# A hybrid attention and recurrence block on one core: the first attention head's loads and scores put within the last pair of block products, and the recurrence values of all heads made during the attention and kept in DRAM

## The chip, the core and the metric

The kernel runs on one core of a Trainium2 chip. Five engines work from instruction queues of their own: TensorE (PE) multiplies matrices, VectorE (DVE), ScalarE (ACT) and GpSimd (POOL) work element by element, and SyncE (SP) issues transfers; POOL issues transfers as well. Each queue runs in order: an instruction that waits holds all that stands behind it on its engine. The metric is the time of one execution on the device in microseconds (us), the median of several runs.

## What is computed

One residual block on an input x of 1024 tokens by 1024 channels, in float32 (RMS norms, reshapes and heads are cut here):

```python
xn = rmsnorm(x, norm1_g)
u = xn @ w_in                      # 5632 columns
q_sb, k_sb, v_sb, f_raw, i_hg, q_hg, g_hg, gate_sb, gate_hg = split(u)
# stick-breaking attention, 8 heads of 64: z = q.k/8, strictly causal
w = exp(log_sigmoid(z) + sum over later keys before t of log(1 - sigmoid(z)))
o_sb = w @ v_sb
# HGRN2 recurrence, 4 heads of 128
f = lb + (1 - lb) * sigmoid(f_raw);  k = 1 - f
S_t = diag(f_t) S_{t-1} + k_t i_t^T;  o_t = S_t^T silu(q_t)
o_hg = rmsnorm(o_hg) * silu(g_hg)
merged = sigmoid(gate_sb + b) * (o_sb @ w_o_sb) + sigmoid(gate_hg + b) * (o_hg @ w_o_hg)
h = x + merged @ w_out
h = h + relu(rmsnorm(h) @ w_ff1)**2 @ w_ff2
out = rmsnorm(h, final_g)
```

## The kernel before, in words

Every float32 operand of a product is split into a high and a low part (names ending in h and l), and a product is made of three matmuls: high by high, low by high, high by low. Some large products are made of seven block products instead of eight. TensorE has most of the work, so the kernel is arranged to give it something to do at any moment.

In order of time, with the profile's microseconds:

1. **Start, 0 to 45.** Eight token blocks of x are loaded and normalised (`norm1`): ACT sums the squares, POOL raises them to the power (line 249 scales the sum `n_ss`, line 253 raises it: `n_y`), DVE multiplies x by it (line 640), TensorE transposes (`xnt`, line 134), and DVE makes the low parts `xnl` (line 335). `early_whole(0, nc.gpsimd)` adds four high and low parts of the first half into `xw` on POOL (line 785), 128x1024 each; `early_whole(1, nc.vector)` does the second half on DVE. Between them the stream `front` makes the first queries and keys (`pjqk`) and the attention values (`pjv`); jobs up to `j_first`, then up to `j_v`.
2. **Block products, 45 to 155.** The queries and keys of the remaining heads, in four `ProjPair` objects of seven block products each (m1, m2, m6, m5, m7, m4, m3; 12 matmuls of 128x512 each; PSUM tiles `ppX`, `ppY`). ACT and DVE split their results into `qkh` and `qkl`, and POOL stores these in DRAM (line 705).
3. **Attention, 155 to 376.** 8 heads of 8 query blocks, 64 items. `qk_load` reads a head's keys `KS` and queries `QH`, `QL` from DRAM by SP (line 139). `v_load` reads its values and the values shifted by one row into `vr` by POOL (line 676); `v_split` subtracts them on DVE (line 685) and splits the difference into `V`. For each item `scores` makes `z` (TensorE), `weights` makes `rm` (sigmoid on ACT, line 946, and a scan on DVE, line 972), `turn` transposes the weights on TensorE (`pw`) and splits them (ACT `wTh`, line 1020; DVE `wTl`, line 1026), and `values` multiplies by `V` (`po`). The scores of an item are issued two items ahead. Between items fill is issued: first the rest of `front`, then steps of a second stream `st`, whose jobs stand in a fixed order. `n_fill = 3 + 7 + 2 * 9 + 17` steps are spread evenly over the 64 items. In `st` the first jobs are raw gate columns (`pga`, `pgq`, with the weights `wga0`), then the recurrence queries, values and gates of head 0.
4. **Recurrence, 376 to 646.** For each of four heads `hg_levels` builds decayed products level by level (DVE multiplies `k`, `q` and `pp`; TensorE makes `sl`, `pk`), and `hg_tail` of the head before carries the state (`fc`, `pkv`, `pho`, `pot`). After each step of either, `st.advance` issues `FILL[h]` steps, 3.75, 3.3, 2.8, 2.6 and 3 for the phases 0 to 4. Fill here is the projections of the other heads, then the output products `pys`. `i_job(h)` makes the recurrence values i of heads h and h+1: 192 matmuls of 128x256 (`pji`), which ACT copies into the slots `v`. Before, `i_job(0)` runs in the attention and `i_job(2)` in the recurrence.
5. **Gates, output and MLP, 646 to 1504.** `gates` starts with `gX`, then come `out_start` (`pwW`), and the MLP.

What sets the order around the change is the sequence written out in the main function. It issues for the last pair `o` (the one with no `n` behind it):

```python
        o.m7()
        if n:
            n.m1()
            n.split_sums()
        else:
            qk_load(0)
            v_load(0)
            front.advance(3, j_v)
        o.m4()
        o.m3()
    v_split(0)
    scores(*items[0])
    weights(*items[0])
    front.advance(2, j_v)
    scores(*items[1])
```

Of the kernel before, what the change touches and what calls it, by code (L numbers as in the profile page):

```python
# [14 lines left out]
ALU = mybir.AluOpType  # L15
# [4 lines left out]
P = 128  # L20
T = 1024
# [4 lines left out]
HGW = 512  # L26
# [13 lines left out]
def kernel(  # L40
# [19 lines left out]
    nc = tc.nc  # L60
# [14 lines left out]
    def slot(name, dt=F32):  # L75
        return spool.tile([P, 1024], dt, tag="s", name=name)
# [11 lines left out]
    def dram(name, shape):  # L88
        return scratch.tile(shape, F32, tag=name, name=name)

    def half(name, dt=F32):
        return hpool.tile([P, 512], dt, tag="h", name=name)
# [15 lines left out]
    def after(ins, earlier):  # L108
        if earlier is not None and earlier.ins is not ins.ins:
            tc.add_manual_dep(ins.ins, earlier.ins.name, NOSYNC, reason="issue order")  # L110
        return ins
# [160 lines left out]
    last_power = [None]  # L272
# [261 lines left out]
    st, front = Stream(), Stream()  # L534
# [50 lines left out]
    def wide_unit(name, mat, c0):  # L585
        return Unit(
            name,
            [
                [
                    (  # L590
                        0,
                        256,
                        mat[k * 512 : (k + 1) * 512, c0 : c0 + 256].rearrange(
                            "(k p) c -> p k c", p=P
                        ),
                    )
                ]
                for k in range(2)
            ],
            wide=True,  # L600
        )
# [47 lines left out]
    def first_row():  # L649
        zero = half("vzero")[0:1, :]  # L650
        nc.gpsimd.memset(zero, 0.0)
        nc.gpsimd.dma_start(vrows[0:1, :], zero)
# [20 lines left out]
    def v_load(h):  # L673
        vraw[h] = slot(f"vr{h}")
        for i, cs in halves():
            nc.gpsimd.dma_start(
                vraw[h][:, cs].rearrange("p (t d) -> p t d", d=DHS),
                vrows[1 - i : T + 1 - i, h * DHS : (h + 1) * DHS].rearrange(
                    "(t p) d -> p t d", p=P
                ),  # L680
            )
# [27 lines left out]
    def qk_load(h):  # L709
        qk[h] = QH, QL, KS = tuple(slot(f"{n}{h}", F32R) for n in ("QH", "QL", "KS"))  # L710
        hi, lo = qkd[h, "h"], qkd[h, "l"]
        q, k = slice(0, DHS), slice(DHS, P)
        for t, r, src in (
            (KS, q, hi[k]), (QH, q, hi[q]), (KS, k, lo[k]), (QH, k, hi[q]), (QL, q, lo[q]),
            (QL, k, lo[q]),
        ):
            load(t[r].bitcast(F32), src)
# [63 lines left out]
    def early_whole(half_, engine):  # L781
        for kp in range(KT // 2):
            h, l = (t.bitcast(F32) for t in xn.t[half_, kp])
            early[half_, kp // 2, kp % 2] = t = slot(f"xw{half_}{kp}")
            engine.tensor_tensor(out=t, in0=h, in1=l, op=ALU.add)

    early_forms = {}

# [139 lines left out]
    def scores(h, qb):  # L928
        open_block("main")
        nk = (qb + 1) * P  # L930
        QH, QL, KS = qk[h]
        rm = slot_n(f"rm{h}_{qb}", nk)
        step = 320 if nk == 640 else 512
        for s0 in range(0, nk, step):
            m = min(nk - s0, step)
            n = max(m, 256)
            z = bank(f"z{h}_{qb}_{s0}")
            for i, Q in enumerate((QH, QL)):
                matmul(
                    z[:, :n],  # L940
                    Q[:, qb * P : (qb + 1) * P],
                    KS[:, s0 : s0 + n],
                    start=i == 0,
                    stop=i == 1,
                )
            nc.scalar.activation(rm[:, s0 : s0 + m], z[:, :m], AF.Sigmoid, scale=-0.125)  # L946
        zs[h, qb] = rm
# [123 lines left out]
    def f_epilogue(h):  # L1071
# [15 lines left out]

        return ep

    def i_job(h):  # L1090
        unit = wide_unit(f"wi{h}", W_IN, C_I + h * P)

        def ep(ps, tb):
            for j in range(2):
                if tb == 0:
                    hg[h + j, "v"] = slot(f"v{h + j}")
                nc.scalar.copy(hg[h + j, "v"][:, tb * P : (tb + 1) * P], ps[:, j * P : (j + 1) * P])

        unit.late = h == 0

        def body():
            for i, _ in enumerate(token_steps(f"pji{h}", unit, xn, range(NT), ep)):
                yield
                if unit.late and i == 6:
                    hi_behind[0] = turn_hi[0]
                    st.prefetch()
                    hi_behind[0] = None

        return st.add([unit], body)

    def silu_epilogue(h, key):
        def ep(ps, half):
# [8 lines left out]
    def hg_job(h, key):  # L1121
        c0, ep = {
            "f": (C_F, f_epilogue), "q": (C_QH, lambda h: silu_epilogue(h, "q")),
            "g": (C_GH, lambda h: silu_epilogue(h, "g")),
        }[key]
        if key == "g" and h % 2 == 0:
            i_job(h)
        u = cols_unit(f"w{key}{h}", [(W_IN, c0 + h * P, P)])
        j_hg[h] = proj_jobs([(f"pj{key}{h}", u, ep(h))], xn)

# [37 lines left out]
    def chunks(t):  # L1168
        return t.rearrange("p (c t) -> p c t", t=P)
# [406 lines left out]

    j_raw = [raw_job(0)]
    hg_job(0, "q")
    hg_job(0, "g")
    j_first_hg = j_hg[0]  # L1580
    for h in range(1, NHG):
# [730 lines left out]
    norm_transpose(xn, 0, 2, 2)  # L2312
    front.advance(5, 1)
    norm1(range(4, NT))
    early_whole(0, nc.gpsimd)
    front.advance(4, 1)
    norm_transpose(xn, 1, 0, 4)
    turns["on"] = False
# [1 line left out]
    lower_bounds()  # L2320
    front.advance(11, j_first)
    first_row()
    early_whole(1, nc.vector)
    early_sums()
    blocks = [qk_parts(h) for h in range(1, NHS)] + [(((C_F, P),), f_epilogue(0))]
# [7 lines left out]
    for o, n in zip(proj, proj[1:] + [None]):  # L2333
        o.m2()
        if n:
            n.load()
        o.m6()
        o.m5()
        if n:
            n.split_plain()  # L2340
        o.m7()
        if n:
            n.m1()
            n.split_sums()
        else:
            qk_load(0)
            v_load(0)
            front.advance(3, j_v)
        o.m4()
        o.m3()  # L2350
    v_split(0)
    scores(*items[0])
    weights(*items[0])
    front.advance(2, j_v)
    scores(*items[1])

    n_fill = 3 + 7 + 2 * 9 + 17
    n_first = 0
    ready = deque()
    wsums = out_weight_sums()  # L2360
# [41 lines left out]
    for h in range(NHG + 1):  # L2402
        lev = hg_levels(h) if h < NHG else iter(())
        tail = hg_tail(h - 1) if h > 0 else iter(())
        upto = (j_hg[2], j_hg[3], j_raw[6], j_sb[1], j_sb[3])[h]
        going = True
        while going:
            going = False
            for g in (lev, tail):
                if next(g, StopIteration) is not StopIteration:  # L2410
                    going = True
                    owed += FILL[h]
                    st.advance(int(owed), upto)
                    owed -= int(owed)
        if h + 1 < NHG:
            st.finish(j_hg[h + 1])
        if h > 1:
            a_hg.put(h - 2, ohg[h - 2], hg_level[0])
# [102 lines left out]
```

## Time and profile before

| what | value |
|---|---|
| median of 3 runs | 1504.18 us (1503.21 to 1505.15) |
| the profiled execution's own time | 1505.72 us |
| its span | 1504.0 us |
| TensorE busy | 1444.2 us, 96% |
| VectorE busy | 1101.0 us, 73% |
| ScalarE busy | 658.6 us, 44% |
| GpSimd busy | 171.9 us, 11% |
| granted TensorE clock, mean | 0.982 of full speed |

The profile's times are those of one execution, in microseconds from the span's start; the 1.7 us between the span and the execution's time lie outside the program's instructions. A row of the timeline gives start, duration, engine, line, operation, output<-inputs, and in brackets how long the engine had been idle before it and what ended that. A row of the windows gives the busy time of each engine in a stretch and the granted TensorE clock (PEclk; 0.50 is half speed).

### The profile page before, as it was taken

How to read it: one execution, taken by the hardware profiler on the slowest of the kernel's cores; microseconds unless marked ns; L12 is line 12 of the kernel's file. 1: busy time of each engine (PE TensorE's matmuls, PEld its weight loads, DVE VectorE, ACT ScalarE, POOL GpSimd, SP SyncE). 2: the span in 40 equal slices, each digit the busy share in tenths (PEclk: the TensorE clock that was granted, in tenths of full speed). 3: DMA queues.
4: the chain of work that ended last, by engine and by line, in shares of the span. 5: the costliest groups of instructions: out<-in, count | busy, mean ns of one | idle time of the engine just before them, and what ended most of it. 6: DMA issues, size and time to landing. Idle time of an engine off the chain costs nothing. (4 is left out here: it accounts for less than half of the span.)

```text
span 1504.0 us, 19848 instructions
## 1 busy us (share of the span) xinstructions
PE 1444.2 (96%) x7422; PEld 1227.2 (82%) x7422; DVE 1101.0 (73%) x1538; ACT 658.6 (44%) x1080; POOL 171.9 (11%) x310
## 2 busy tenths in 40 slices
PE   7999679999999999999998999999999999999998
PEld 7988668897889888888886888888888888888886
DVE  5964568888964779887875889766666756859756
ACT  5443346655231334443333475444444534343433
POOL 5212212131000011210001030000000000000032
PEclk9999888999999999999999999999999999999999
DMA  5255655674121144874448652444444886666835
GB/s 196 85 147 168 154 155 138 136 140 92 43 91 30 54 108 152 234 231 154 150 158 256 227 182 79 139 154 154 154 155 154 310 315 235 222 236 244 286 109 192
DMA packets 164729, 248.80 MB, mean 165 GB/s; under 512 B 26860, under 2 KB 95000, under 8 KB 164632
## 3 DMA queue, kind: packets, MB, share of 16 engines
q1 hardware_dynamic: 146392, 195.87, 40.2%
q0 software_dynamic: 14496, 45.10, 10.9%
q10 hardware_dynamic: 3744, 6.56, 1.2%
q8 instruction: 58, 0.95, 0.3%
q14 instruction: 39, 0.32, 0.1%
HBM read 179.33 MB, written 72.35 MB: 167 GB/s over the span
## 5 line engine op out<-in xcount | busy, mean ns | idle before, releaser
L154 ACT CAST whid<-w 128x1024 fp32r<-128x1024 f32 x30 | 31.6, 1055 | 153.6 <-PE pm L131 85.8
L972 DVE TENSOR_TENSOR_SCAN rm<-rm,bits 128x512 f32<-128x512 f32 (+6 forms) x72 | 87.5, 1224 | 11.6 <-ACT rm L946 11.4
L131 PE MATMUL pm<-whid,sh 128*128 128x512 f32 x240 | 93.4, 389 | 0.0
L131 PE MATMUL pm<-wlod,sh 128*128 128x512 f32 x240 | 93.4, 389 | 0.0
L131 PE MATMUL pm<-whid,sl 128*128 128x512 f32 x240 | 93.4, 389 | 0.0
L131 PE MATMUL pm<-tl,sh 128*128 128x512 f32 (+1 forms) x210 | 81.3, 387 | 0.0
L131 PE MATMUL pm<-th,sl 128*128 128x512 f32 (+1 forms) x210 | 81.3, 387 | 0.0
L131 PE MATMUL pm<-th,sh 128*128 128x512 f32 (+1 forms) x210 | 81.3, 387 | 0.0
L159 DVE TENSOR_TENSOR wlod<-w,whid 128x1024 fp32r<-128x1024 f32 x30 | 36.7, 1224 | 57.5 <-ACT whid L154 57.5
L159 DVE TENSOR_TENSOR sl<-sa,sh 128x1024 fp32r<-128x1024 f32 x56 | 68.3, 1220 | 0.7 <-ACT sh L154 0.7
L2132 POOL TENSOR_SCALAR fss<-fss 128x1 f32<-128x1 f32 x8 | 4.4, 553 | 562.1 <-ACT fsc L2127 561.6
L1020 ACT ACTIVATE wTh<-pw,minus_one 128x128 fp32r<-128x128 f32 (+3 forms) x96 | 54.2, 587 | 27.4 <-PE pw L134 25.0
L154 ACT CAST sh<-sa 128x1024 fp32r<-128x1024 f32 x56 | 57.3, 1048 | 6.1 <-DMA sa<-ad 6.1
L134 PE MATMUL pw<-ident,rm 128*128 128x128 f32 x288 | 46.4, 286 | 11.9 <-DVE rm L972 11.9
L1026 DVE SCALAR_TENSOR_TENSOR wTl<-pw,wTh 128x128 fp32r<-128x128 f32 (+3 forms) x96 | 50.6, 546 | 9.7 <-ACT wTh L1020 9.3
L131 PEld LDWEIGHTS pm<-wlod,sh 128*128 128x128 f32 x240 | 45.1, 188 | 9.4
L131 PEld LDWEIGHTS pm<-whid,sl 128*128 128x128 f32 x240 | 45.0, 188 | 9.4
L131 PEld LDWEIGHTS pm<-whid,sh 128*128 128x128 f32 x240 | 45.1, 188 | 9.3
L134 PEld LDWEIGHTS pw<-ident,rm 128*128 128x128 f32 x288 | 36.8, 148 | 16.8 <-DVE rm L972 12.6
L131 PE MATMUL po<-wTh,V 128*128 128x256 f32 x160 | 45.5, 312 | 5.1 <-DVE wTl L1026 3.3
L131 PE MATMUL pX<-sql,t1h 128*128 128x512 f32 x128 | 50.0, 391 | 0.1
L131 PE MATMUL pX<-sqh,t1l 128*128 128x512 f32 x128 | 49.8, 389 | 0.0
(963 smaller groups left out, 4613.4 us busy)
## 6 DMA issues: line engine op xcount, KB each, us to landing
w<-in_w_ff_dram SPq DMA_DIRECT2D x72, 512.0 KB, 5.1
sa<-ad SPq DMA_DIRECT2D x56, 512.0 KB, 6.2
ad<-a SPq DMA_DIRECT2D x32, 256.0 KB, 4.2
ad<-s SPq DMA_DIRECT2D x16, 512.0 KB, 5.9
tw<-in_w_out_dram POOLq DMA_DIRECT2D x24, 256.0 KB, 5.2
x<-in_x_dram SPq DMA_DIRECT2D x8, 512.0 KB, 8.7
qkh<-qkh POOLq DMA_DIRECT2D x16, 256.0 KB, 3.2
qkl<-qkl POOLq DMA_DIRECT2D x16, 256.0 KB, 3.2
```

Of the source, the lines that this page charges most:

```text
L131: return pe(nc.tensor.matmul(*a, **k))
L134: return pe(nc.tensor.transpose(dst, src, ident))
L154: hi_last[0] = after(in_turn("act", nc.scalar.copy(dst, src)), hi_behind[0])
L159: nc.vector.tensor_tensor(out=dst, in0=src, in1=hi.bitcast(F32), op=ALU.subtract),
L972: sc = nc.vector.tensor_tensor_scan(out=rr, data0=rr, data1=bits[:, 1024 - nk + a : 1024 - nk + b][:, ::-1], initial=rm[:, b : b + 1] if i ...
L1020: nc.scalar.activation(th[:, 0:n, qs], src, AF.Identity, bias=minus_one),
L1026: nc.vector.scalar_tensor_tensor(out=tl[:, 0:n, qs], in0=src, scalar=-1.0, in1=th[:, 0:n, qs].bitcast(F32), op0=ALU.add, op1=ALU.subtract,),
L2132: nc.gpsimd.tensor_scalar(out=ssq, in0=ssq, scalar1=1.0 / D, scalar2=EPS, op0=ALU.mult, op1=ALU.add)
```

## The change

Three things are changed.

- `early_whole(0, nc.gpsimd)`, POOL's four additions `xw`, is called later, behind `first_row()`, and each is ordered behind POOL's last power step (`last_power`).
- For the last pair, `qk_load(0)` and `v_load(0)` stand behind m6 instead of m7, the first item's `scores` and `weights` stand between m4 and m3, and all that is left of the attention values (`front`) is issued behind m3, around the scores of the second item.
- Both `i_job` calls stand in `st` behind the first head's recurrence queries. An `i_job` no longer copies into the slots `v`: ACT copies a 128x256 result into one half of a 128x512 tile, and POOL stores each full tile in the DRAM tensor `irows` (8 stores of 256 KB). A new `i_load(h - 1)` reads one head's values back (512 KB, POOL) at the start of phase h. `n_fill` goes from 45 to 59; `FILL` stays.

```diff
         for kp in range(KT // 2):
             h, l = (t.bitcast(F32) for t in xn.t[half_, kp])
             early[half_, kp // 2, kp % 2] = t = slot(f"xw{half_}{kp}")
-            engine.tensor_tensor(out=t, in0=h, in1=l, op=ALU.add)
+            after(engine.tensor_tensor(out=t, in0=h, in1=l, op=ALU.add), last_power[0])
...
+    irows = dram("irows", [T, HGW])
+
     def i_job(h):
         unit = wide_unit(f"wi{h}", W_IN, C_I + h * P)
+        pair = {}
 
         def ep(ps, tb):
-            for j in range(2):
-                if tb == 0:
-                    hg[h + j, "v"] = slot(f"v{h + j}")
-                nc.scalar.copy(hg[h + j, "v"][:, tb * P : (tb + 1) * P], ps[:, j * P : (j + 1) * P])
+            i, c = tb // 2, tb % 2 * 256
+            if c == 0:
+                pair[i] = half(f"i{h}_{i}")
+            nc.scalar.copy(pair[i][:, c : c + 256], ps)
+            if c:
+                rows_ = irows[i * 256 : (i + 1) * 256, h * P : (h + 2) * P]
+                nc.gpsimd.dma_start(
+                    rows_.rearrange("(t p) c -> p t c", p=P),
+                    pair.pop(i).rearrange("p (t c) -> p t c", t=2),
+                )
...
+    def i_load(h):
+        hg[h, "v"] = slot(f"v{h}")
+        nc.gpsimd.dma_start(
+            chunks(hg[h, "v"]),
+            irows[:, h * P : (h + 1) * P].rearrange("(t p) c -> p t c", p=P),
+        )
...
-        if key == "g" and h % 2 == 0:
-            i_job(h)
...
     hg_job(0, "q")
+    i_job(0)
+    i_job(2)
     hg_job(0, "g")
...
     norm1(range(4, NT))
-    early_whole(0, nc.gpsimd)
     front.advance(4, 1)
...
     first_row()
+    early_whole(0, nc.gpsimd)
     early_whole(1, nc.vector)
...
         o.m6()
+        if not n:
+            qk_load(0)
+            v_load(0)
         o.m5()
...
-        else:
-            qk_load(0)
-            v_load(0)
-            front.advance(3, j_v)
         o.m4()
+        if not n:
+            scores(*items[0])
+            weights(*items[0])
         o.m3()
     v_split(0)
-    scores(*items[0])
-    weights(*items[0])
-    front.advance(2, j_v)
+    front.advance(4, j_v)
     scores(*items[1])
-
-    n_fill = 3 + 7 + 2 * 9 + 17
+    front.advance(5, j_v)
+
+    n_fill = 7 + 2 * 9 + 2 * 17
...
+        if h > 0:
+            i_load(h - 1)
```

The rows below, of POOL at the start of the program, are the first place at which the order differs. `n_5`, `n_6`, `n_7` are the token blocks 5 to 7; `_ss` and `_y` are the two steps of the power. Before:

```order
L253 TENSOR_TENSOR n_5_y<-n_5_ss,expo 128x1
L785 TENSOR_TENSOR xw_474<-xnh_245,xnl_246 128x1024
L249 TENSOR_SCALAR n_6_ss<-n_6_ss 128x1
L785 TENSOR_TENSOR xw_476<-xnh_253,xnl_254 128x1024
L253 TENSOR_TENSOR n_6_y<-n_6_ss,expo 128x1
L249 TENSOR_SCALAR n_7_ss<-n_7_ss 128x1
L785 TENSOR_TENSOR xw_478<-xnh_261,xnl_262 128x1024
L253 TENSOR_TENSOR n_7_y<-n_7_ss,expo 128x1
L785 TENSOR_TENSOR xw_480<-xnh_269,xnl_270 128x1024
L705 DMA qkh_99<-qkh_0_482 128x512
```

The same place on POOL in the changed kernel:

```order
L253 TENSOR_TENSOR n_5_y<-n_5_ss,expo 128x1
L249 TENSOR_SCALAR n_6_ss<-n_6_ss 128x1
L253 TENSOR_TENSOR n_6_y<-n_6_ss,expo 128x1
L249 TENSOR_SCALAR n_7_ss<-n_7_ss 128x1
L253 TENSOR_TENSOR n_7_y<-n_7_ss,expo 128x1
L705 DMA qkh_99<-qkh_0_475 128x512
L705 DMA qkl_100<-qkl_0_476 128x512
L666 DMA vrows<-v_1_518 128x2x256
L785 TENSOR_TENSOR xw_750<-xnh_246,xnl_247 128x1024
L785 TENSOR_TENSOR xw_752<-xnh_254,xnl_255 128x1024
L785 TENSOR_TENSOR xw_754<-xnh_262,xnl_263 128x1024
L785 TENSOR_TENSOR xw_756<-xnh_270,xnl_271 128x1024
```

The four additions no longer stand between the power steps of the token blocks 5 to 7; they stand behind three stores.

The second place is DVE around the first head's `vr`, at the end of the block products (`pv` is a sum of block products, `k` and `pp` belong to the forget gate, `qkl_1` is a low part to be stored, `rm_7` the first item's weights, `rm_0` and `rm_6` the next items'; the scans of line 972 are called SCALAR_TENSOR_TENSOR here and TENSOR_TENSOR_SCAN in the profile). Before:

```order
L882 TENSOR_TENSOR pv_1562<-pu_1355,ppY_1445 128x512
L1076 TENSOR_SCALAR k_1475<-k_1475,oml 128x512
L1079 TENSOR_SCALAR pp_1474<-pp_1474,oml,lb 128x512
L685 TENSOR_TENSOR vr_1489<-vr_1489 128x512
L972 SCALAR_TENSOR_TENSOR rm_0_1610<-rm_0_1610,bits 128x128
L159 TENSOR_TENSOR V_1569<-vr_1489,V_1569 128x8x64
L972 SCALAR_TENSOR_TENSOR rm_7_1572<-rm_7_1572,bits 128x512 x2
L972 SCALAR_TENSOR_TENSOR rm_6_1616<-rm_6_1616,bits 128x896
```

In the changed kernel:

```order
L882 TENSOR_TENSOR pv_1485<-pu_1483,ppY_1458 128x512
L685 TENSOR_TENSOR vr_1455<-vr_1455 128x512
L1076 TENSOR_SCALAR k_1488<-k_1488,oml 128x512
L1079 TENSOR_SCALAR pp_1487<-pp_1487,oml,lb 128x512
L159 TENSOR_TENSOR qkl_1_1506<-ppX_1343,qkh_1_1505 128x512
L972 SCALAR_TENSOR_TENSOR rm_7_1511<-rm_7_1511,bits 128x512
L159 TENSOR_TENSOR V_1541<-vr_1455,V_1541 128x8x64
L972 SCALAR_TENSOR_TENSOR rm_7_1511<-rm_7_1511,bits 128x512
L882 TENSOR_TENSOR pv_1534<-pu_1356,ppY_1458 128x512
```

The subtraction `vr` stands behind the sum of m7's result instead of the one of m3's, ahead of `k`, `pp` and `qkl_1`; the first item's scans come directly behind, ahead of m3's `pv`. On POOL the load of `vr` now stands ahead of the stores of `qkh_1` and `qkl_1`, which belong to m4; before, it stood behind them. On PE the two score matmuls `z_7` with `QH` stand directly behind m7 and those with `QL` behind m4.

The third place is TensorE near the end of the last recurrence head's levels (`pys` are the output products that serve as fill; `sl_6` is the last level, `pk` the transposes that follow). Before:

```order
L131 MATMUL pys_0_6047<-asbh_5959,wo00h_5899 128x512
L131 MATMUL pys_0_6047<-asbl_5960,wo00h_5899 128x512
L131 MATMUL pys_0_6047<-asbh_5959,wo00l_5900 128x512
L134 MATMUL pk_0_6069<-ident,k_5141 128x128 x4
L134 MATMUL pk_1_6075<-ident,k_5141 128x128 x3
```

In the changed kernel:

```order
L131 MATMUL pys_1_6122<-asbh_5869,wo01h_5899 128x512
L131 MATMUL pys_1_6122<-asbl_5870,wo01h_5899 128x512
L131 MATMUL pys_1_6122<-asbh_5869,wo01l_5900 128x512
L131 MATMUL sl_6_6169<-q_5176,k_5065 64x64 x8
L134 MATMUL pk_0_6193<-ident,k_5065 128x128 x4
L134 MATMUL pk_1_6199<-ident,k_5065 128x128 x3
```

Before, 12 `pys` matmuls stand between `sl_6` and `pk_0`; in the changed kernel there are none. Between the last transposes `pot` and the first `gX` stand 78 `pys` matmuls before and 12 in the changed kernel.

## The prediction on record

> **What bounds the kernel now.** I read the page first. The span is 1504.0 us and TensorE is busy for all but 60 us of it:
>
> ```profile
> span 1504.0 us, 19848 instructions
> ...
> PE 1444.2 (96%) x7422; PEld 1227.2 (82%) x7422; DVE 1101.0 (73%) x1538; ACT 658.6 (44%) x1080; POOL 171.9 (11%) x310
> ```
>
> So an edit gains only where TensorE waits or where its clock is low. The windows by stage, in which the columns behind the span are the busy times of TensorE, its weight loads, VectorE, ScalarE and GpSimd, say where that is:
>
> ```profile
> core 0: us, PE busy (x) PEld busy (x) DVE busy (x) ACT busy (x) POOL busy (x), PEclk, DMA share, GB/s
> 0.00:45.00 45.00, 33.42 (x237) 31.98 (x238) 26.94 (x40) 25.65 (x50) 23.41 (x38) 0.89 0.58 188
> 45.00:74.00 29.00, 29.00 (x221) 27.81 (x220) 28.61 (x37) 13.97 (x22) 4.33 (x7) 1.00 0.26 73
> 74.00:155.00 81.00, 81.00 (x378) 67.86 (x378) 43.78 (x58) 31.17 (x45) 16.53 (x30) 1.00 0.51 151
> 155.00:206.00 51.00, 32.42 (x195) 28.88 (x195) 33.02 (x44) 22.73 (x48) 9.66 (x25) 0.82 0.52 132
> 206.00:376.00 170.00, 154.81 (x1009) 138.89 (x1009) 141.38 (x203) 100.23 (x222) 39.63 (x91) 0.95 0.64 138
> 376.00:417.00 41.00, 41.00 (x242) 34.45 (x241) 37.80 (x86) 10.71 (x17) 0.00 (x0) 1.00 0.14 39
> 417.00:490.00 73.00, 73.00 (x504) 66.14 (x504) 42.29 (x87) 20.47 (x54) 3.07 (x5) 1.00 0.20 62
> 490.00:559.00 69.00, 69.00 (x396) 58.53 (x395) 48.69 (x97) 21.52 (x45) 5.75 (x7) 1.00 0.25 69
> 559.00:622.00 63.00, 61.27 (x362) 52.00 (x361) 57.01 (x103) 24.53 (x47) 12.97 (x16) 1.00 0.70 194
> 622.00:664.00 42.00, 42.00 (x215) 35.54 (x214) 35.49 (x44) 20.88 (x40) 7.78 (x11) 1.00 0.61 206
> ```
>
> TensorE is idle for 11.6 us in 0–45, 18.6 us in 155–206 and 15.2 us in 206–376. Those are also the stretches with a granted clock below 1.00. The block products (74–155) and the recurrence (376–664) leave it next to nothing, and the MLP isn't touched by the change. The summary of TensorE's waits names the causes:
>
> ```profile
> PE pw L134 <- DVE rm L972: 11.9, 2, 11.2
> ...
> PE xnt L134 <- DVE x L640: 7.5, 2, 5.4
> ...
> PE pga L131 <- ACT wga0whi L154: 4.9, 1, 4.9
> ...
> PE pgq L131 <- ACT wga0t L154: 1.8, 1, 1.8
> ...
> PE sl L131 <- DVE pp L167: 1.7, 1, 1.7
> ...
> PE pga L131 <- DVE wga0wlo L159: 0.8, 1, 0.8
> ```
>
> Behind the long waits the clock halves. The windows show 0.50 or 0.51 there:
>
> ```profile
> 163.80:174.10 10.30, 3.24 (x15) 3.24 (x16) 6.21 (x7) 3.33 (x7) 0.00 (x0) 0.50 0.99 250
> 191.10:198.00 6.90, 5.83 (x19) 4.66 (x20) 5.41 (x8) 0.95 (x2) 0.00 (x0) 0.51 0.25 74
> 204.80:208.20 3.40, 3.40 (x9) 2.62 (x10) 1.95 (x3) 1.12 (x2) 0.00 (x0) 0.51 0.68 223
> 34.10:44.40 10.30, 4.88 (x22) 4.61 (x23) 7.39 (x7) 3.34 (x5) 7.08 (x6) 0.50 0.29 89
> ```
>
> A stretch at half clock loses half of TensorE's busy time in it: 1.6, 2.9, 1.7 and 2.4 us.
>
> **Startup.** These are GpSimd's rows around the additions `xw`, and VectorE's for the token blocks that wait for the power `n_y`:
>
> ```profile
> 27.25 2.41 POOL L785 TENSOR_TENSOR xw<-xnh,xnl 128x1024 f32<-128x1024 f32 x1
> ...
> 30.34 2.37 POOL L785 TENSOR_TENSOR xw<-xnh,xnl 128x1024 f32<-128x1024 f32 x1
> ...
> 34.13 2.34 POOL L785 TENSOR_TENSOR xw<-xnh,xnl 128x1024 f32<-128x1024 f32 x1
> 36.43 0.55 POOL L253 TENSOR_TENSOR n_y<-n_ss,expo 128x1 f32<-128x1 f32 x1
> 36.94 2.34 POOL L785 TENSOR_TENSOR xw<-xnh,xnl 128x1024 f32<-128x1024 f32 x1
> ```
>
> ```profile
> 33.25 0.75 DVE L640 TENSOR_SCALAR x<-x,n_y 128x1024 f32<-128x1024 f32 x1 [3.04 <-POOL n_y L253]
> 37.01 2.82 DVE L640 TENSOR_SCALAR x<-x,n_y 128x1024 f32<-128x1024 f32 x1 [3.01 <-POOL n_y L253]
> ```
>
> Block 7's `n_y` comes at 36.43 because three rounds of `xw` (2.41, 2.37 and 2.34 us) stand ahead of it on GpSimd. Without them it comes 7.1 us earlier, before TensorE asks for it (34.1, where its half-clock window begins), so both waits for `x` (7.5 us) go and the half-clock loss (2.4 us) with them. The upper bound of the gain is 9.9 us; VectorE must still normalise the blocks one behind another at 0.75 us, so I take 9 as the gross gain.
>
> What is late next is `xw` itself. Its four additions, 4 x 2.36 = 9.4 us, now run beside VectorE's low parts and half-1 sums. The normalisation at 37.01 took 2.82 us beside an `xw`, and the same operation at 33.25 took 0.75 us: those two did not overlap at all. Behind it, in 45–74, VectorE is busy 28.61 of 29.00 us, so what it loses there TensorE loses too. Bounds: hold of 0 (gain 9) to all of 9.4 (loss 0.4). The pair of rows shows it for one operation only; whether the low parts and the sums are held like it, no row shows. In 0–45 VectorE is busy 26.9 us of 45, so a part of a hold falls into time that it has free. I take a hold of 3, a third: **−6 (−9 to +0.5)**.
>
> The Trainium skill, SBUF — State Buffer, section "Who interferes with whom", says that a VectorE operation with at most one SBUF input, outside its two-port modes, does not contend with GpSimd, while one with two SBUF inputs shuts out a GpSimd read. By it the low parts hide about two of the four `xw`, and two, 4.7 us, are left as hold: a gain of about 4 and a sum of 1475. No run here shows it yet.
>
> **The first stall, 11.2 us before `pw`.** GpSimd's queue, VectorE's wait, two rows of TensorE (the first matmul behind m7, and the first transpose of weights), SyncE's issues, and the times from issue to landing of `vr`:
>
> ```profile
> 153.13 0.54 POOL L705 DMA_DIRECT2D qkh<-qkh  x1 [13.24 <-ACT qkh L154]
> ...
> 154.39 1.80 POOL L676 DMA_DIRECT2D vr<-vrows  x2
> ```
>
> ```profile
> 167.22 0.69 DVE L685 TENSOR_TENSOR vr<-vr 128x512 f32<-128x512 f32 x1 [9.84 <-DMA vr<-vrows]
> ```
>
> ```profile
> 144.94 0.28 PE L131 MATMUL pjv<-wv1h,xnh 128*128 128x256 f32 x1
> ```
>
> ```profile
> 170.86 0.90 PE L134 MATMUL pw<-ident,rm 128*128 128x128 f32 x3 [11.15 <-DVE rm L972]
> ```
>
> ```profile
> 138.33 0.52 SPq L139 DMA_DIRECT2D KS<-qkh  x1
> 139.47 0.45 SPq L139 DMA_DIRECT2D QH<-qkh  x1
> ```
>
> ```profile
> DMA to landing us min/median/max: 3.8/9.0/11.5
> ```
>
> GpSimd waited 13.24 us for ScalarE's `qkh` of m4 and only then issued `vr` (154.39). VectorE stood at the subtraction until 167.22 with the first head's scans behind it, and TensorE at `pw` until 170.86. In the changed kernel `vr` stands ahead of that store. It waits only for m6's buffers, so it can issue at about 140 and lands, by the slowest load (11.5 us), at 151.5. Scores come at m7's end (144.9). After them TensorE has m4 and m3, 24 matmuls of 0.22 us (74–155: 378 in 81.0 us), 5.3 us, and 96 `pjv` matmuls of half that size, 10.6 us: until about 161. From the subtraction to `pw` it took 3.6 us (167.22 to 170.86), so even the slowest `vr` has the weights ready by 156, with some 5 us to spare. The stall goes whole, with its half clock: 11.2 + 1.6 = **−12.8 (−5 to −12.8)**. The cover are those `pjv`; without them the wait would come back by the part that `vr` lands behind 151. The upper end takes that in.
>
> The price is a new wait: `z_7` stands on TensorE directly behind m7 with m4, m3 and the `pjv` queued behind it. The keys leave at 138.33 and the queries at 139.47, already as early as m6's buffers come free. No row shows these loads under a wait at this place; the nearest is `vr`, 3.8 to 11.5 us. From 139.5 that ends between 143 and 151, and TensorE asks at 144.9: 0 to 6 us. Whole rows of keys should be nearer to the fast end, so I take **+1 (0 to +6)**.
>
> **The second stall.** `wga0`'s waits (4.9, 0.8 and 1.8 us) and the half clock behind them (2.9 and 1.7) come from ScalarE's cast of weights whose load SyncE issued behind both heads' keys and queries, and whose split stood behind the first head's work. The changed SyncE order has `wga0` ahead of the second head's keys, and the splits run behind m3's sum. **−12 (−8 to −12).** Ends: all, or the half clock of the last part stays.
>
> **The rest of the attention.** 206–376 loses 15.2 us idle and 5% of 154.8 at low clock, 22.9 in all. Into it comes the second `i_job`:
>
> ```profile
> L131 PE MATMUL pji<-wi2h,xnh x64: 277/283/366, 452.8 to 481.7; 128*128 128x256 f32 x64
> ```
>
> Three such groups of 64 matmuls are 192; at half of 0.22 to 0.24 us, for half the columns, they are 21 to 23 us, and I take 22. Fill goes from 45 to 59 steps, so there are more matmuls between an item's transposes and its products. VectorE has 141.4 us in this stretch and TensorE 147 + 22 = 169 at full clock (154.8 x 0.95, and the new ones), so TensorE stays the bound, with VectorE at 83%. The waits won't all go: many are one item's chain. I let a little over half remain: **−10 (−3 to −16)**, apart from the moved work. The eight stores to `irows` stand on GpSimd in front of the memory sets for later items; those are issued well ahead of use, so nothing for them.
>
> **The recurrence and the gates.** The 22 us leave this stretch, where TensorE was busy for 286 of 288 us; that only returns if VectorE's chain lets TensorE go faster. VectorE's busy time is 37.8 of 41, 42.3 of 73, 48.7 of 69, 57.0 of 63: the phases of heads 1 and 2 have room, head 3's has none. With equal `FILL` the stock is used up earlier. Before, output products were left over:
>
> ```profile
> 645.95:663.76 17.81, 17.81 (x81) 14.72 (x80) 15.05 (x18) 8.10 (x10) 2.24 (x4) 1.00 0.75 248
> ```
>
> That block of 17.8 us, TensorE alone, covered the sums for the gates. In the changed kernel it is 12 matmuls, 2.7 us; the sums now run beside head 3's levels, on a VectorE that is full there. By the order's count at 0.22 us each TensorE has some 54 us there, against 57–59 of VectorE: +4. No fill stands between `sl_6` and `pk`: +2 (a like wait, `sl` on `pp`, cost 1.7). One half-clock window behind such waits: +1. The last head's values, 512 KB from DRAM by GpSimd, wait for a buffer that VectorE frees only behind that head's levels, and `pkv` asks for them soon after; nearest are `vr`'s 3.8 to 11.5 us, of which some 3 to 5 are covered, so +1.5 (0 to +6), nearer to the short end. Sum **+8.5 (+3 to +16)**.
>
> The Trainium skill, DMA: Bandwidth & Descriptors, section "Anatomy of one DMA", gives 2.0 us plus bytes by 436 GB/s for such a load, an estimated 3.2 us here; by it the last term would be 0. The `vr` row (9.0 us at the median for half the bytes) disagrees.
>
> **The sum.** −6 − 12.8 + 1 − 12 − 10 + 8.5 = −31.3 us. Against the profiled execution, 1505.72 us, that is 1474.4; the median lies 1.5 us below that execution, so 1473.
>
> **The rivals.**
>
> - *`xw` holds VectorE for all its 9.4 us* (for: the 2.82 us row; against: a hold of `xnl` isn't shown). The start gains nothing: 1479. Chance 0.15.
> - *The recurrence gives most back.* With the fill thinner, every phase waits for its own chain of levels; for: 57.0 of 63 busy, 17.8 us of cover gone; against: no waits in 417–559 before. The stretch keeps its length, +22 instead of +8.5: 1486. Chance 0.15.
> - *Everything is taken*: start 9, attention 16, recurrence +3 gives 1459. Chance 0.10.
> - *The early loads are not early.* The keys already left at 138.33, and `vr` could wait for something else on its queue; the first stall stays: 1486. Chance 0.05.
> - *Slower.* GpSimd's queue stops at each `irows` store until ScalarE's copy, as it did 13.24 us for `qkh`, and the next head's `vr` stands behind. Each head hit would pay what the first stall did, 12.8 us. Below two heads the change still gains; from three on (38 us) it is slower than before: 1511, and with four 1524. Against: the loads are issued a head ahead. Chance 0.05.
>
> The forecast itself, within 1465 to 1480, has 0.50. About 0.2% (3 us) is what a measurement of this kernel can tell from no change; only mixtures of the last three rivals come near it. So faster 0.92, same 0.03, slower 0.05. The range, 1459 to 1488, reaches over the second and third rival.
>
> **What would show it.** Right: TensorE's waits list no `x`, no `wga0` and no `rm` over 2 us; `vr` issues near 140 less what the start gained; PEclk is 1.00 up to 206; 622–664 loses its block of `pys`. The steps fail one by one if `z<-QH` shows over 2 us, if VectorE's `xnl` or sums last over twice as long as before beside `xw`, if `sl`, `pk` or `pkv` waits over 10 us in sum. The forecast is wrong altogether if `po` and `pw` wait as long as before with the fill denser.

## The result, and the profile after

The changed kernel takes 1493.72 us (median of 4 runs, 1493.46 to 1495.09) against 1504.66 us before (1503.21 to 1509.27): a ratio of 0.9924, 95% interval 0.9901 to 0.9946. It is faster by 11 us, where 31 were forecast, and lies above the range of 1459 to 1488. The profiled execution took 1493.49 us, its span 1491.8 us.

The page's first lines:

```profile
span 1491.8 us, 19878 instructions
...
PE 1440.0 (97%) x7422; PEld 1223.7 (82%) x7422; DVE 1106.6 (74%) x1538; ACT 656.4 (44%) x1064; POOL 177.2 (12%) x322
```

TensorE is idle for 51.8 us of the span, 8 us less than before, and its mean clock rose from 0.982 to 0.985, by estimate worth 4 us of its 1440. The summary of its waits names other causes than before; the columns are the wait, the total, the number and the longest:

```profile
PE ppar L215 <- DVE xnl L335: 9.0, 1, 9.0
PE z L131 <- DMA QH<-qkh: 8.0, 2, 4.4
...
PE sl L131 <- DVE pp L167: 4.0, 1, 4.0
PE po L131 <- ACT wTh L1020: 3.7, 3, 1.9
PE pw L134 <- ACT i L1100: 3.5, 1, 3.5
PE po L131 <- DVE wTl L1026: 2.7, 5, 1.0
PE pgq L131 <- ACT wga0t L154: 2.5, 1, 2.5
...
PE pk L134 <- DVE k L167: 1.4, 1, 1.4
```

The two big stalls at the attention's head (`rm` 11.2 us, `wga0whi` 4.9 us) are gone, and `xnt` on `x` (7.5 us) as well. The many short waits of `po` for `wTl` went from 9.9 us, in this row of before, to 2.7:

```profile
PE po L131 <- DVE wTl L1026: 9.9, 13, 3.3
```

In the place of all these stand one wait of 9.0 us for `xnl`, two for queries (8.0 us together), one for ScalarE's copy `i` (3.5 us). The windows by stage, to be read against those of before:

```profile
0.00:45.00 45.00, 32.17 (x241) 30.90 (x242) 31.92 (x40) 27.41 (x53) 24.14 (x38) 0.93 0.62 197
...
155.00:206.00 51.00, 47.37 (x301) 42.08 (x301) 38.09 (x51) 28.52 (x58) 13.31 (x31) 0.97 0.59 165
206.00:376.00 170.00, 155.66 (x1118) 145.24 (x1117) 134.00 (x186) 99.24 (x213) 42.37 (x94) 0.97 0.63 137
...
417.00:490.00 73.00, 73.00 (x413) 61.59 (x411) 45.19 (x91) 20.16 (x43) 5.63 (x7) 1.00 0.26 80
...
559.00:622.00 63.00, 57.72 (x339) 48.37 (x337) 57.91 (x97) 25.85 (x48) 13.56 (x18) 0.97 0.74 203
```

The start still loses as much as before (12.8 us idle of 45, 11.6 before). 155–206 lost only 3.6 us instead of 18.6, while 206–376 still has 14.3 us idle, 15.2 before, at a clock of 0.97 instead of 0.95. In the recurrence only the phase of the last head (559–622) waits, and there VectorE is busy 57.9 of 63.

For the comparison of all kernels I cut the span at three places that every profile shows: the last matmul of m7 in the last pair, the first `sd` (the recurrence begins), and the first `gX`. The forecast by the same stages is worked out from its terms: −6 for the start, −12.8 + 1 − 12 − 10 + 22 for the attention, −22 + 8.5 for the recurrence.

| kernel | start to m7's end | attention | recurrence to gX | rest | median, us |
|---|---|---|---|---|---|
| before | 144.9 | 230.8 | 288.1 | 840.2 | 1504.66 |
| forecast | 138.9 | 219.0 | 274.6 | 840.2 | 1473 |
| after | 145.6 | 235.1 | 271.6 | 839.5 | 1493.72 |

The recurrence came out as forecast, 3 us better. The start missed its 6 us and the attention 16 us. Those two are what the experiments are about.

### The profile page after: what moved, and what is told of

It reads as the page before. It is cut to its first block, busy times and chain, and to the rows that moved or that the text cites. A ratio compares the mean times of both kernels' runs of the same rounds, so it can differ in the third digit from the quotient of the medians.

```text
span 1491.8 us, 19878 instructions
## 1 busy us (share of the span) xinstructions
PE 1440.0 (97%) x7422; PEld 1223.7 (82%) x7422; DVE 1106.6 (74%) x1538; ACT 656.4 (44%) x1064; POOL 177.2 (12%) x322
## 5 line engine op out<-in xcount | busy, mean ns | idle before, releaser
L1020 ACT ACTIVATE wTh<-pw,minus_one 128x512 fp32r<-128x512 f32 (+2 forms) x96 | 53.4, 585 | 24.7 <-PE pw L134 23.9
L1026 DVE SCALAR_TENSOR_TENSOR wTl<-pw,wTh 128x512 fp32r<-128x512 f32 (+2 forms) x96 | 49.9, 545 | 7.5 <-ACT wTh L1020 6.9
L131 PE MATMUL pX<-sqh,t1h 128*128 128x512 f32 x128 | 49.8, 389 | 0.0
L946 ACT ACTIVATE rm<-z 128x512 f32<-128x512 f32 (+3 forms) x96 | 44.0, 492 | 6.4 <-PE z L131 4.2
```

What stands on the lines that cost most here:

```text
L131: return pe(nc.tensor.matmul(*a, **k))
L1020: nc.scalar.activation(th[:, 0:n, qs], src, AF.Identity, bias=minus_one),
L1026: nc.vector.scalar_tensor_tensor(out=tl[:, 0:n, qs], in0=src, scalar=-1.0, in1=th[:, 0:n, qs].bitcast(F32), op0=ALU.add, op1=ALU.subtract,),
```

## The experiments

**Theories.** For the start: the four additions `xw`, now back to back on GpSimd, hold one VectorE operation with two operands in SBUF, `wv1l`, and everything behind it in VectorE's queue. These are the rows of GpSimd, VectorE and TensorE of the changed kernel:

```profile
32.70 9.25 POOL L785 TENSOR_TENSOR xw<-xnh,xnl 128x1024 f32<-128x1024 f32 x4
```

```profile
29.71 0.75 DVE L640 TENSOR_SCALAR x<-x,n_y 128x1024 f32<-128x1024 f32 x1 [0.72 <-POOL n_y L253]
...
30.98 12.05 DVE L159 TENSOR_TENSOR wv1l<-wv1r,wv1h 128x1024 fp32r<-128x1024 f32 x2
42.96 4.03 DVE L335 SCALAR_TENSOR_TENSOR xnl<-xnt,prm,xnh 128x512 fp32r<-128x512 f32 x6
```

```profile
43.75 0.32 PE L215 MATMUL ppar<-ident,prow 36*128 36x36 f32 x1 [9.01 <-DVE xnl L335]
```

The last normalisation begins at 29.71, as the forecast had it, 7.3 us earlier than before (37.01). Then two `wv1l` take 12.05 us instead of the 2.35 that the same pair took before. GpSimd runs `xw` from 32.70 to 41.95, and VectorE is free again at 43.0, one `wv1l` later. The low parts `xnl` stand behind it, and TensorE waits 9.01 us for them. The pair in the profile of before:

```profile
40.35 2.35 DVE L159 TENSOR_TENSOR wv1l<-wv1r,wv1h 128x1024 fp32r<-128x1024 f32 x2
```

The rival was that GpSimd's reads hold every VectorE operation, so that no order of these would help.

For the attention: the stalls that the last pair's part removes are truly gone, but the denser fill moves its own weight loads to moments at which they hold a queue. The rival was that TensorE is simply full there.

**The cause of the start.** In the changed kernel, one small read of `wv1l` by GpSimd is put ahead of `xw`:

```diff
     first_row()
+    g0 = small.tile([P, 1], F32, tag="g0", name="g0", bufs=1)
+    w = front.jobs[j_v - 1][0][0].hl[1][1].bitcast(F32)[:, 0:1]
+    last_power[0] = nc.gpsimd.tensor_tensor(out=g0, in0=w, in1=w, op=ALU.add)
     early_whole(0, nc.gpsimd)
```

> The changed kernel with one small addition on GpSimd that reads VectorE's low part wv1l ahead of the four additions xw, so that these start only when wv1l is done. Theory (the four xw in a row hold the VectorE operation that reads two operands from SBUF, here the second wv1l, 10.9 us instead of 1.2, and the low parts xnl queue behind it): wv1l takes 1.2 us, the xnl rows run beside xw at their own 0.7 us, TensorE's wait of 9.0 us before ppar falls below 1, and the time is 6 to 8 us below the changed kernel's, 1486 to 1488. Rival (GpSimd's reads hold every VectorE operation): the hold moves to xnl, the wait stays at 7 us or more, the time stays at 1493 within 1.5.

Its rows on GpSimd and VectorE:

```profile
36.26 9.43 POOL L785 TENSOR_TENSOR xw<-xnh,xnl 128x1024 f32<-128x1024 f32 x4
```

```profile
32.84 2.35 DVE L159 TENSOR_TENSOR wv1l<-wv1r,wv1h 128x1024 fp32r<-128x1024 f32 x2
35.11 4.04 DVE L335 SCALAR_TENSOR_TENSOR xnl<-xnt,prm,xnh 128x512 fp32r<-128x512 f32 x6
...
43.15 2.58 DVE L226 TENSOR_TENSOR lmx<-prm 128x4 f32<-128x4 f32 x1
```

`wv1l` takes 2.35 us for two again, and six `xnl` run in 4.04 us, 0.67 each, the later four beside `xw`: these are not held. Only `lmx`, a tiny operation with two operands in SBUF, is held, 2.58 us until `xw` ends at 45.7. The 9.0 us wait is gone, and m7 ends at 140.5 instead of 145.6, although the later token blocks came 1.9 us later in this execution (the normalisation of block 4 began at 27.17 instead of 25.31). So the theory holds. The time, 1490.84 us (1486.87 to 1492.42; ratio to before 0.9916, 0.9889 to 0.9944), is 3 us below the changed kernel's, less than the 6 to 8 expected, and doesn't by itself separate the two; the trace does. In its profiled execution, the slowest of the four, the recurrence and the rest took 3.6 us longer than in the changed kernel. A later pair of kernels that differs by this edit alone, 1480.06 and 1474.47, agrees; another, 1485.55 and 1482.19, differs by the move of `xw` as well.

**The three parts alone.** Each is put into the kernel before by itself; the edits are hunks of the change's diff.

The move of `xw`:

> The kernel before with only the move of the four additions xw. Theory: the whole gain of the start is eaten by the hold of wv1l, so the time is that of before within 2 us, 1503 to 1506. Rival (my forecast's term, a third of the hold costs): 6 us faster, 1498.

It took 1503.26 us, ratio 0.9999 (0.9979 to 1.0019), and m7 ends at 145.2; TensorE's wait of 9.0 us for `xnl` is there too. The part gains nothing: theory.

The part on the last pair, with `n_fill = 7 + 2 * 9 + 17`:

> The kernel before with only the part on the last pair (loads behind m6, first scores between m4 and m3, attention values behind m3; 42 fill steps in place of 45, since three steps are made earlier). Theory: this part carries nearly all of the gain; the stalls of 11.2 us and 4.9 us go, a wait of some 3 us for the first queries and one of 2 us for wga0t come: 12 to 18 us below before, 1486 to 1492. Rival (it is the denser fill that removes the stalls): at most 8 us below before, 1496 or more.

It took 1485.55 us, ratio 0.9891 (0.9864 to 0.9918): 19 us faster than before, a little more than the 12 to 18 expected, and 8 us faster than the whole change. Its attention lasts 210.0 us instead of 230.8, and what is left of its waits is small and spread:

```profile
PE po L131 <- DVE wTl L1026: 10.8, 14, 1.4
...
PE pgq L131 <- ACT wga0t L154: 2.3, 1, 2.3
...
PE z L131 <- DMA QH<-qkh: 1.4, 1, 1.4
```

The forecast had −12.8 + 1 − 12 = −23.8 for this part, and 20.8 came.

The part on the recurrence values, with `n_fill = 3 + 7 + 2 * 9 + 2 * 17`:

> The kernel before with only the part on the recurrence values (both jobs in the attention, through DRAM, 62 fill steps). Theory (the denser fill pays in the attention with late loads what it saves in the recurrence): within 4 us of before, 1500 to 1508, with waits for QH or weights of 3 us and more in the attention. Rival (the forecast: waits of the attention filled, recurrence shorter by most of what moved): 10 us below before or more, 1494 or less.

It took 1503.44 us, ratio 0.9995 (0.9980 to 1.0010): nothing gained. The attention grows by 13.2 us to 244.0, which is the moved 22 us less 9, and the recurrence shrinks by 16.0. The terms are near the forecast's (10 and 13.5). By these, +12 and −13.5, this part alone was worth only 1.5 us, so the result agrees with the forecast's sum; the 10 us that the expectation puts down to the forecast aren't in it. The long waits are still there, and `wTh` has grown from 1.7 us to 6.3:

```profile
PE pw L134 <- DVE rm L972: 10.4, 1, 10.4
...
PE po L131 <- ACT wTh L1020: 6.3, 3, 2.8
PE pga L131 <- ACT wga0whi L154: 5.5, 1, 5.5
```

The sign of the theory, waits of 3 us and more for `QH` or for weights that weren't there before, didn't come: TensorE's list has no wait for queries, and `wga0whi` cost 4.9 us before.

So the parts alone give −1, −19 and −1 us, while together they give −11. Put on top of the last pair's part, the values cost the attention 25.1 us (210.0 to 235.1), all of what moved and 3 us more, instead of the 12 of the forecast. Something stands there that neither part has alone.

**What stands there.** The changed kernel's rows of SyncE, with the landing times of the queries:

```profile
200.27 1.50 SPq L139 DMA_DIRECT2D wi2r<-in_w_in_dram  x2
201.94 0.45 SPq L139 DMA_DIRECT2D KS<-qkh  x1
202.48 0.65 SPq L139 DMA_DIRECT2D QH<-qkh  x1
```

```profile
DMA to landing us min/median/max: 3.5/5.7/12.4
```

The rows of ScalarE and TensorE behind them, and two windows:

```profile
270.79 1.04 ACT L154 CAST wg0h<-wg0r 128x1024 fp32r<-128x1024 f32 x1 [6.78 <-DMA wg0r<-in_w_in_dram]
```

```profile
272.16 0.55 PE L134 MATMUL pw<-ident,rm 128*128 128x128 f32 x3 [3.51 <-ACT i L1100]
```

```profile
200.00:210.00 10.00, 10.00 (x66) 9.00 (x65) 8.67 (x14) 6.06 (x14) 2.78 (x7) 1.00 0.95 231
...
270.00:280.00 10.00, 6.42 (x30) 6.02 (x31) 6.83 (x10) 5.43 (x12) 3.05 (x9) 0.69 0.08 27
```

The second job's weights `wi2r`, 1 MB in two loads, leave at 200.27 directly ahead of head 2's keys and queries, in a window where the DMA engines are 95% busy; a load of `QH` takes up to 12.4 us, and TensorE waits 4.40 us for it at 216.36. Later ScalarE has the cast `wg0h` in its queue 6.78 us ahead of its data, with a copy `i`, a cast `V` and the `wTh` of an item behind it; TensorE waits 3.51 us, then 1.4 us, and runs at half clock behind that (0.69 in 270–280; 0.50 from 273.9 to 280.3, where it is busy for 5.6 us and so loses 2.8). With the values alone neither stands: there `wi2r` left 8 us ahead of the next head's keys, and ScalarE waited 0.30 us at `wg0h`. Two kernels take one cause each, or both.

The second values job behind the gates:

```diff
     i_job(0)
-    i_job(2)
     hg_job(0, "g")
-    j_first_hg = j_hg[0]
+    i_job(2)
+    j_first_hg = len(st.jobs)
```

> The changed kernel with the second values job behind the first head's recurrence gates in the order of the fill (queries, values of heads 0 and 1, gates, values of heads 2 and 3), so that one weight load of 512 KB, not two, stands on SyncE ahead of the keys and queries of head 2. Theory (the denser fill brings its weight loads into the same moments as the next head's queries, and the split of wg0 holds ScalarE until its load lands): the waits of 4.4 us for QH of head 2 and of 3.5 us for ScalarE's i fall below 1.5 us each, and with the half clock behind them the time is 5 to 9 us below the changed kernel's, 1485 to 1489. Rival (the added matmuls themselves are the cost, TensorE is simply full): 1492 to 1495.

```profile
PE po L131 <- DVE wTl L1026: 4.3, 7, 1.1
...
PE z L131 <- DMA QH<-qkh: 3.0, 2, 2.9
...
PE z L131 <- DMA QL<-qkl: 1.2, 1, 1.2
```

```profile
DMA to landing us min/median/max: 3.6/4.7/9.4
```

It took 1480.06 us, ratio 0.9841 (0.9818 to 0.9864), 14 us below the changed kernel: more than the 5 to 9 expected. No wait for `i` is left, and head 2's queries cost 1.4 us, 1.2 for `QL` and 0.2 for `QH`; of the 3.0 us for `QH`, 2.9 are the first head's. TensorE is idle 12.3 us in the attention instead of 21.6, at a clock of 1.00 instead of 0.96; 219.5 us is the forecast's 219.0. TensorE was not full; the rival falls.

The second cause alone, the preparation of the next weights put six steps into either job:

```diff
-        unit.late = h == 0
+        unit.late = True
```

> The changed kernel with the preparation of the next weights put six steps into the second values job as well, so that ScalarE's split of wg0 stands behind later attention work; the load order on SyncE ahead of head 2 is as in the changed kernel. Theory: the wait of 3.5 us for ScalarE's i and the 1.4 us behind it go, with their half clock 5 us: 1487 to 1490; the wait of 4.4 us for QH of head 2 stays. Rival (another instruction holds ScalarE's queue in its place): 1492 to 1495.

It took 1485.18 us, ratio 0.9876 (0.9849 to 0.9904), 2 us below the expected 1487 to 1490. The hold of ScalarE is gone, the wait for head 2's queries stays, 4.5 us of these:

```profile
PE z L131 <- DMA QH<-qkh: 4.7, 2, 4.5
...
PE po L131 <- ACT wTh L1020: 1.2, 3, 0.5
```

The attention is 10.2 us shorter. Some 2.2 of these are not the edit's: the first head's queries, ahead of which nothing was changed, cost 1.4 us here (0.3 for `QH`, 1.1 for `QL`) instead of 3.6. The other 8 fit the hold of 3.5 + 1.4 us with the 2.8 lost at half clock behind it.

The load of the first head's `vr` behind m4:

```diff
             qk_load(0)
-            v_load(0)
         o.m5()
...
         o.m4()
         if not n:
+            v_load(0)
```

> The changed kernel with the load of the first head's vr behind m4 instead of directly behind the queries. Theory (vr's transfers share the DMA engines with the first head's queries): z's first wait for QH falls from 3.6 us to 1.5 or less, vr lands by 162, before V is needed at 170, and the time is 2 to 4 us below the changed kernel's, 1490 to 1492. Rival (the queries take their time by themselves): the wait stays at 3 us or more and the time at 1493 to 1495.

The first wait for `QH` is 1.30 us here instead of 3.61, as the theory had it. But in the kernels that leave `vr` directly behind the queries this wait runs from 0.26 us to 3.61, so that `vr` takes the engines from them is not shown. Head 2's wait became 5.21 us, and the time, 1493.26 us (ratio 0.9931, 0.9904 to 0.9957), is that of the changed kernel, as the rival had it:

```profile
146.51 0.73 PE L131 MATMUL z<-KS,QH 128*128 128x512 f32 x2 [1.30 <-DMA QH<-qkh]
```

```profile
212.62 0.77 PE L131 MATMUL z<-KS,QH 128*128 128x512 f32 x1 [5.21 <-DMA QH<-qkh]
```

**The versions that come out of it.** The last pair's part with `xw` behind `wv1l`, without the values:

> The kernel before with the part on the last pair and the move of xw behind wv1l (the small GpSimd read of the first experiment), without the part on the recurrence values. Theory (the parts add, since they stand in different stages: the start 5 to 7 us, the last pair 19): 1477 to 1481. Rival (what the start gains is waited for again at the first queries): 1484 to 1487, with z waiting for QH by 5 us or more.

1482.19 us (1478.97 to 1485.02), ratio 0.9856 (0.9828 to 0.9885); m7 ends at 140.1, and the first `z` waits 0.9 us for `QH`. The start's gain is kept, though the median is 1 us above the 1481 expected at most.

The changed kernel with both corrections:

> The changed kernel with both corrections: xw behind wv1l, and the second values job behind the first gates. Theory (the two holds stand in different stages, 5 us at the start and 14 in the attention): 1473 to 1476, the start up to the end of m7 near 140 us, attention near 219, recurrence near 271. Rival (what the start gains is lost again to the first queries, or the gain of the second was chance): 1479 to 1482.

```profile
PE po L131 <- DVE wTl L1026: 4.4, 7, 1.1
...
PE sl L131 <- DVE pp L167: 4.0, 1, 4.0
PE z L131 <- DMA QH<-qkh: 3.6, 2, 2.0
...
PE pk L134 <- DVE k L167: 1.6, 1, 1.6
```

1474.47 us (1472.73 to 1477.34), ratio 0.9809 (0.9785 to 0.9833): 29 us below before. Its stages are 138.8, 220.6 and 273.2 us, against 138.9, 219.0 and 274.6 of the forecast.

Three kernels go on from this one. The first changes the rates of the fill, so that output products are left for the last head's levels:

```diff
-    FILL = (3.75, 3.3, 2.8, 2.6, 3)
+    FILL = (3.6, 3.0, 2.6, 2.8, 3)
```

> As the kernel before it, with FILL 3.6, 3.0, 2.6, 2.8, 3 in place of 3.75, 3.3, 2.8, 2.6, 3, so that 18 output products stand between sl_6 and pk of the last head, where there were none. Theory (the last head's levels wait only because the fill is used up): the waits sl on pp (4.0) and pk on k (1.4) go, 3 to 6 us below that kernel. Rival (VectorE is the bound of that phase, and the order of the fill doesn't matter): the waits move to other products, within 1.5 us of it.

1477.01 us, ratio 0.9826 (0.9805 to 0.9848), no gain: 2.5 us above the kernel it starts from, where the theory had 3 to 6 below and the rival at most 1.5 off. The wait of 4.0 us for `pp` shrinks to 1.4 and another comes:

```profile
PE pkv L131 <- DMA v<-irows: 3.2, 1, 3.2
...
PE sl L131 <- DVE pp L167: 1.4, 1, 1.4
```

That is the last head's values from DRAM: what doesn't wait at `sl` waits at `pkv`. The theory, that the missing fill alone is the cause, falls; of the rival the part holds that the wait moves on, though it moved to a transfer.

`vr` behind m4, on top of both corrections:

> As e9, with the load of the first head's vr behind m4. Theory: the first wait for QH (2.9 us there) falls to 1.5 or less as it did in the kernel with this edit alone, and now it pays: 1 to 2 us below e9. Rival: vr, later, makes VectorE's first scans late, and the time stays or rises by up to 2 us.

1474.88 us, ratio 0.9813 (0.9789 to 0.9837). The first wait for `QH` goes from 1.98 us to 0.24, the time does not move by more than the measurement tells. The next kernel, which leaves `vr` ahead, has 0.37 us there, so this wait doesn't settle it either.

The values kept in SBUF instead of DRAM (ScalarE copies into the slots `v` as before, both jobs still in the attention):

> As e9, but the values stay in SBUF: ScalarE copies 128x128 pieces into the four slots v as before the change, nothing goes through DRAM. Theory (the trip through DRAM is free, its stores have no one waiting behind them and its loads land in 6 us at most): within 2 us of e9. First rival (the trip costs transfers that slow the next head's queries): 3 us or more below e9. Second rival (four more slots held in the attention make loads wait for buffers): 5 us or more above e9.

1484.85 us, ratio 0.9882 (0.9855 to 0.9908), 10 us above the kernel with DRAM:

```profile
PE z L131 <- DMA QL<-qkl: 6.1, 3, 4.0
```

One wait for `QL` late in the attention, at 334, is 3.98 us, and TensorE is idle 17.7 us in the attention instead of 11.9. So the trip through DRAM is not what it costs; it pays, as the second rival had it. Its reason, that loads wait for the slots, wasn't shown by itself; what the trace shows is that `QL` takes 10.6 us at the median to land here, and 7.0 in the kernel with DRAM.

## Why the prediction was wrong, step by step

- **The start, −6: wrong.** The failed step is "I take a hold of 3, a third". The normalisations did come 7 us earlier, and both waits for `x` went; the wait of 9.0 us for `xnl` that came in their place brought a half clock of its own (0.50 in 45–48). The hold was not 3 us but 9.7 (12.05 − 2.35), and one operation took all of it. I looked at how much of VectorE's work would fall beside `xw` and not at which operation heads its queue there: `wv1l`, two operands in SBUF, with all the low parts behind it. The rival with the full hold (chance 0.15) was the right one. The Trainium skill, SBUF — State Buffer, section "Who interferes with whom", had the right distinction, and the first experiment agrees with it: 0.67 us per `xnl` beside `xw`, and 2.58 us for the tiny `lmx`. I read it as a share of the time, 4.7 us, where it names the operations.
- **The first stall, −12.8, and the second, −12: right, together 3 us short.** 11.2 and 4.9 us are gone, and `vr` left at 140.61; the last pair's part alone took 20.8 us from the attention, where 23.8 were forecast with the new wait. Of that wait, +1 (0 to +6), 3.61 us came in the changed kernel, over the 2 us named as a sign of failing, and 1.42 with this part alone. `wga0t` still costs 2.5 us.
- **The rest of the attention, −10: wrong.** The mechanism was right: the waits of `po` for `wTl` fell from 9.9 us to 2.7. The failed step is that the added fill was taken as matmuls alone. It has weights: `wi2r` came ahead of head 2's queries, and the cast of `wg0` ahead of its data. I had moved the jobs' matmuls through the order and not their loads and splits. The kernel with the order turned has an attention of 219.5 us instead of 235.1: 15.6 us, nearly the whole miss of 16.
- **The recurrence, +8.5 of the 22: right, and a little too dear.** 271.6 us against a forecast of 274.6: the waits came where they were put, `sl` for `pp` 4.0 us and `pk` for `k` 1.4 us. The last values' load did not wait here; with the fill shifted it did, 3.2 us, inside the 0 to +6 given. The Trainium skill's DMA: Bandwidth & Descriptors, section "Anatomy of one DMA", gives 2.0 us plus bytes by 436 GB/s, an estimated 3.2 us for such a load. The four loads here took longer, 5.1 us at the median.
- **The rival on the other side** had its mechanism: GpSimd did stop at each store to `irows` until ScalarE's copy, 74.4 us in sum. The row is from GpSimd's idle time before its transfers to and from `irows`, by what ended it. TensorE's list shows no wait that came of it: none for `V`, and 0.3 us for `rm`.

```profile
  ACT i L1100: 74.4, 8
```

- **The sum.** With both holds removed the kernel takes 1474.5 us, 1.5 us from the number forecast, and every stage is within 2 us. The attention and the recurrence were sized well; two holds of in-order queues, both caused by instructions that the change moved along, were missing or too small. That the start fits as well is in part luck: its −6 is a gain of 9 less a hold of 3, and with the hold of `wv1l` gone 6.2 us came, not 9, and 4.3 to 4.8 in the five other kernels with this correction.

What stays open: what sets the first head's wait for `QH`, 0.26 to 3.61 us; why `QL` lands later with the values in SBUF; and at which moment `wv1l` was shut out, since its recorded start, 32.1, lies 0.6 us ahead of the first `xw`, and a store that GpSimd issued at 31.95 stands between.

## What to carry to other kernels

When work is moved, move its loads, splits and stores through every queue as well, and ask of each what it will stand in front of; a step of fill is not only matmuls. When an engine is freed from one order and its work is put back to back elsewhere, look up which single operation at the other engine meets it, since in an in-order queue one held operation is the whole queue. Take the parts of a change apart on the chip: here one part alone was worth 19 us, and the whole 11.

## What the runs showed of the hardware

- A VectorE operation with two operands in SBUF was held for a whole run of four GpSimd operations, 10.9 us for one `wv1l`, and not let in between two of them. One with an operand in PSUM ran beside them at its own 0.67 us. Two operands aren't needed for a hold: before, the normalisation of a token block, which reads one tensor in SBUF and a column of scalars, took 2.82 us beside an `xw` and 0.75 alone.
- The clock halved behind short waits too: behind TensorE's wait of 2.51 us for `wga0t` the clock granted was 0.50 in 179.0–181.5, and behind those of 3.51 and 1.4 us it was 0.50 from 273.9 to 280.3.
- One kind of load, 256 KB of `QH`, took 3.5 to 12.4 us to land in one kernel. In the four kernels with both loads of `wi2r` ahead of head 2's queries the slowest took 12.1 to 13.2 us, in those with `wg0r` alone ahead 9.4 to 10.8.
